# A hybrid decoder layer on one core: first projections by kinds of parts, other buffers for held weights, evictions behind weight splits, and half banks in the last product

## The chip, the cores and the metric

The kernel runs on one core of a Trainium2 chip. The metric is device time in microseconds, the median over several runs. Five engines work side by side, each on its own queue of instructions in program order: TensorE (PE, matmuls and transposes; PEld is its weight load), VectorE (DVE), ScalarE (ACT), GpSimd (POOL) and SyncE (SP, which here only issues DMAs). They wait for each other by semaphores.

## The reference

One layer with a residual stream of 1024 rows of 1024 columns, with 16 learned rows put ahead of it. All is float32.

```python
u = rmsnorm(h, g_pre_mix)
z = u @ w_in                                   # q | k | v | x_rec | y_rec
attn = sliding_window_attention_with_sinks(q, k, v, sinks)      # window 128, 8 heads, 2 kv heads
xr = causal_depthwise_conv(xr, conv_w, conv_b)
hr = rg_lru(xr, w_a, b_a, w_x, b_x, lru_lambda)
rec = gelu(yr) * hr
h = h + rmsnorm(concat([attn, rec]) @ w_out, g_post_mix)
u = rmsnorm(h, g_pre_ffn)
f = square(relu(u @ w_ff1)) @ w_ff2            # 1024 -> 4096 -> 1024
h = h + rmsnorm(f, g_post_ffn)
return h[:, 16:]
```

## The kernel before

**Parts.** Every float32 operand of a matmul is split into a high part (rounded to the matmul's type by ACT, L95 or L116) and a low part (the remainder, by DVE, L98 or L117). A product is three matmuls: high by high (L123), high by low (L124), low by high (L125), all added up in a PSUM bank (`mm3`). The high part of a weight is ready before its low part, since DVE subtracts what ACT wrote.

**Start.** The rows come in four pieces (`ALL`: 272 rows with the 16 learned ones, then three times 256). For each piece `normed` takes the norm (a square with a sum on ACT, L200; two steps on POOL, L158 and the power L164; a multiply on DVE, L202), `transposed` turns it on TensorE into PSUM (L242) and splits it into `u`, and `project` runs the K, V, Q and X columns over it. The results go to sinks: `sink_k` copies K into two arrangements, with casts on ACT (L303) and DVE (L304) and subtractions on DVE (L305). The projections' accumulators take turns on two banks with the tag acc, so a third projection waits until the first one's sink has read its bank. `kl` is zeroed in part by POOL (L298).

**Middle.** Attention, with the other projections placed between its steps (50 to 250 us in the trace), then the recurrence's gates, then the output projection.

**Feed-forward, first product.** Both big products are done by a recursive scheme of seven half-size products in place of eight, with sums and differences of blocks of the weights taken on DVE (`combine`, L789). In `prep_a` piece p loads two blocks of w_ff1, r0 (tag raw) and r1 (tag d, four buffers), takes sums, splits, and writes r1 to DRAM (`s_dram`, by POOL, L834) for a later pass (`fetch_b`). A d buffer is free again only when that write is done. Another operand, t4, is written to DRAM too (L963) and loaded into `ot4` (L1015) for the third pass.

**Feed-forward, second product.** `steps` are 56 pairs (i, q): seven products of eight steps each; a step is 24 matmuls of 512 columns. Step n runs while `prep_2` makes the operands of step n + 1 and `fetch_2` loads w_ff2 for step n + 3 into the tags raw and e (two buffers each). Where the weight is a sum of two blocks, the second one is added either by an accumulating DMA, issued by POOL (L1039), or it is loaded by SP too (L1042) and added by DVE:

```python
if len(wx) == 3 and wx[2] is ADD and raws and (i < 6 or q % 2 == 0):
    nc.gpsimd.dma_start(raws[0], w2v[q, a, b], accum_op=ADD)
    break
```

After each product `evict` adds the four banks to sums in SBUF (L1144, L1147, L1149) in the first four steps of the next product. `finish_early` ends the lower rows (L1094 squares, L1101 scaling, an accumulating DMA from h_dram at L1105). `finish_half` prepares half the columns of the upper rows in the first four steps of the last product. The last three steps (`LAST`) are run row block by row block, and `finish_late` ends each: eviction (L1126), squares on ACT (L1094), L160 and the power L164, a multiply by the gain (L1129), two scalings with the residual (L1131) and two output DMAs (L1134).

**What sets the order.** A scheduler orders each engine's queue by priorities and by its own estimate of the times; `behind(name, ins)` adds an order of one instruction after another on the same engine without a semaphore. `mark` and `urgent` are names for it. Slots (`slot`) with one tag take turns on that tag's buffers, and whoever takes one waits for the last reader or writer of the one before.

Of the kernel before, what the change touches and what calls it, by code (L numbers as in the profile page):

```python
# [37 lines left out]
def hybrid_layer(  # L38
# [76 lines left out]
    def split_scaled(hi, lo, src, scale):  # L115
        nc.scalar.activation(hi, src, AF.Copy, scale=scale)  # L116
        nc.vector.scalar_tensor_tensor(  # L117
            lo, src, scale, f32(hi), op0=ALU.mult, op1=ALU.subtract
        )

    def mm3(dst, lhs, rhs, start, stop):
        (lh, ll), (rh, rl) = lhs, rhs
        nc.tensor.matmul(dst, lh, rh, start=start, stop=False, skip_group_check=True)  # L123
        nc.tensor.matmul(dst, lh, rl, start=False, stop=False, skip_group_check=True)  # L124
        nc.tensor.matmul(dst, ll, rh, start=False, stop=stop, skip_group_check=True)  # L125
# [29 lines left out]
    def rstd_of(ssq_parts, n=P):  # L155
        ms = small.tile([P, 1], F32, name="ms", tag="ms")
        if len(ssq_parts) == 1:
            nc.gpsimd.tensor_scalar(ms[:n], ssq_parts[0], EPS, None, op0=ALU.add)  # L158
        else:
            nc.vector.scalar_tensor_tensor(  # L160
                ms[:n], ssq_parts[0], EPS, ssq_parts[1], op0=ALU.add, op1=ALU.add
            )
        rs = small.tile([P, 1], F32, name="rs", tag="rs")
        nc.gpsimd.tensor_tensor(rs[:n], ms[:n], half_pow[:n], op=ALU.pow)  # L164
        return rs[:n]

# [30 lines left out]
    def norm_rows(src, n):  # L197
        xn = slot("d", [P, D])
        ssq = small.tile([P, 1], F32, name="ssq", tag="ssq")
        nc.scalar.activation(xn[:n], src, AF.Square, scale=RMS_SC, accum_out=ssq[:n])  # L200
        rs = rstd_of([ssq[:n]], n)
        nc.vector.tensor_scalar(xn[:n], src, rs, None, op0=ALU.mult)  # L202
        return xn
# [13 lines left out]

    ALL = [(0, 272), (272, 256), (528, 256), (784, 256)]
    REAL2 = [(16, 512), (528, 512)]

# [14 lines left out]
    def transposed(b, xn):  # L235
        t0, n = ALL[b]
        for kc in range(KC):
            flip[0] += 1
            pt = bank(("pt", "o", "s")[flip[0] % 3])
            o = 0  # L240
            for s, m in xn:
                nc.tensor.transpose(  # L242
                    pt[:, o : o + m], s[:m, kc * P : (kc + 1) * P], ident[:m, :m]
                )
                o += m
            uh, ul = u[kc]
            split_scaled(
                uh[:, t0 : t0 + n], ul[:, t0 : t0 + n], pt[:, :n],
                g_mix_col[:, kc : kc + 1],
            )  # L250

# [25 lines left out]
    wk = split_w(rk, "b")  # L277
    wv = split_w(rv, "b")
    transposed(0, xn)
    wq = split_w(rq)  # L280
    wx = split_w(rx)
# [8 lines left out]

    khh = [slot("b", [P, T], F32R) for _ in range(2)]
    kl = [slot("b", [P, T], F32R) for _ in range(2)]

    vk = [slot("b", [P, 8, P], F32R) for _ in range(2)]
    HALF = (slice(0, HD), slice(HD, P))
    vt = slot("c", [P, TT])
    for h in range(2):
        nc.gpsimd.memset(f32(kl[h][HALF[1 - h]]), 0.0)  # L298
# [43 lines left out]

    q0, sink_q0 = new_q()
    xr0, sink_x0 = new_x("c")
    for b in range(4):
        if b:
            transposed(b, normed(b))
        piece = [ALL[b]]
        project(wk, piece, sink_k)
        project(wv, piece, sink_v)  # L350
        project(wq, piece if b else [(16, 256)], sink_q0)
        project(wx, piece, sink_x0)
# [251 lines left out]
    nc.gpsimd.memset(graw, 0.0)  # L604
# [207 lines left out]
    def prep_a(p, late=None):  # L812
        r0 = slot("raw", [P, 4, 256])
        w1_load(r0, 0, p, 0, 2)
        r1 = slot("d", [P, 4, 256])
        w1_load(r1, 1, p, 0, 2)
        a11, a21, a12, a22 = r0[:, :, LO], r0[:, :, HI], r1[:, :, LO], r1[:, :, HI]
        sums = [
            combine(a22, a21, a22, ALU.add), combine(a21, a11, a21, ALU.subtract)
        ]  # L820
        if late:
            behind(late, *sums)
        hi, lo = pair("ws", [P, 4, 256])
        if p in a11_early:
            split(hi[:, :, HI], lo[:, :, HI], a21)
            first = a11_early[p]
        else:
            split(hi, lo, r0)
            first = hi[:, :, LO], lo[:, :, LO]
        combine(a11, a22, a11, ALU.subtract)  # L830
        hl = slot("e", [P, 2, 4, P], F32R)
        split(hl[:, 0], hl[:, 1], a11)
        combine(a12, a12, a11, ALU.subtract)
        nc.gpsimd.dma_start(s_dram[p], r1)  # L834
        return first, (hl[:, 0], hl[:, 1]), (hi[:, :, HI], lo[:, :, HI])
# [177 lines left out]
    for i in range(2):  # L1013
        for n in range(2):
            nc.sync.dma_start(f32(ot4[i][n]), t4_dram[:, n, 2 * i : 2 * i + 2, :])  # L1015

# [15 lines left out]
    def fetch_2(n):  # L1032
# [4 lines left out]
        for (a, b), tag in zip(wx[:2], tags):  # L1037
            if len(wx) == 3 and wx[2] is ADD and raws and (i < 6 or q % 2 == 0):
                nc.gpsimd.dma_start(raws[0], w2v[q, a, b], accum_op=ADD)  # L1039
                break  # L1040
# [5 lines left out]
    def prep_2(n, tag="ws"):  # L1046
# [3 lines left out]
        if len(raws) == 2:  # L1050
            combine(raws[0], raws[0], raws[1], wx[2])
        wh, wl = pair(tag, [P, 2, 512])
        split(wh, wl, raws[0])
# [11 lines left out]
    ready, raw_2 = {}, {}  # L1065


    done = set()
    for n, p in enumerate(third):
# [13 lines left out]
        product(y4, wc[p][1], ot4, True)  # L1083
# [24 lines left out]
    late = {}  # L1108

    def finish_half(j):  # L1110
# [9 lines left out]
        nc.vector.tensor_tensor(o[:, c], acc[:, c], gffn_b[:, c], op=ALU.mult)  # L1120
        late[j] = h, o, ssq

    def finish_late(j, y):
        h, o, ssq1 = late[j]
        acc, c = facc["0", j], COLS[0]
        nc.vector.tensor_tensor(acc[:, c], y, acc[:, c], op=ALU.add)  # L1126
        ssq0 = squares(o[:, c], acc[:, c], 0)
        rs = rstd_of([ssq0, ssq1])
        nc.vector.tensor_tensor(o[:, c], acc[:, c], gffn_b[:, c], op=ALU.mult)  # L1129
        for c in COLS[::-1]:  # L1130
            nc.vector.scalar_tensor_tensor(  # L1131
                o[:, c], o[:, c], rs, h[:, c], op0=ALU.mult, op1=ALU.add
            )
            nc.sync.dma_start(out[j * P : (j + 1) * P, c], o[:, c])  # L1134
# [3 lines left out]
    def evict(i, j, y):  # L1138
        for half, b, sign in PLAN[i][2]:
# [6 lines left out]
            elif sign > 0:  # L1146
                nc.vector.tensor_tensor(dst, y, dst, op=ALU.add)  # L1147
            else:
                nc.vector.tensor_tensor(dst, dst, y, op=ALU.subtract)  # L1149

    def step_mm(accs, j, q, ops):
        fh, fl, wh, wl = ops
        c = slice(j * P, (j + 1) * P)
        for s_ in range(2):
            mm3(
                accs[j], (fh[:, s_, c], fl[:, s_, c]), (wh[:, s_, :], wl[:, s_, :]),
                q == 0 and s_ == 0, q == 7 and s_ == 1,
            )

# [5 lines left out]
    for n, (i, q) in enumerate(steps):  # L1165
        if n + 3 < len(steps):
            raw_2[n + 3] = fetch_2(n + 3)
        if n + 1 < len(steps):
            ready[n + 1] = prep_2(n + 1, "a" if n + 1 >= len(steps) - LAST else "ws")
        if q == 0:  # L1170
            old = None if i == 0 else accs
            accs = [bank(("acc", "s", "pt", "o")[j]) for j in range(4)]
        if n < len(steps) - LAST:
            for j in range(4):
                step_mm(accs, j, q, ready[n])
            del ready[n]
        if old and q < 4:
            evict(i - 1, q, old[q])
# [5 lines left out]
        if i == 6 and q < 4:  # L1184
            finish_half(q)
    for j in range(4):
        for n in sorted(ready):
            step_mm(accs, j, steps[n][1], ready[n])
        finish_late(j, accs[j])
# [31 lines left out]
```

## Time and profile before

| | us |
|---|---|
| median of 3 runs | 995.67 (993.17 to 998.14) |
| profiled execution | 997.85 |
| its span, first to last instruction | 995.9 |
| TensorE busy | 962.2 |
| VectorE busy | 673.5 |
| ScalarE busy | 502.9 |
| GpSimd busy | 76.5 |

The profiled execution is one run; its own time is its span and some 2 us around it. The busy share of TensorE is high everywhere but at a few places, and these are best found by windows of equal length: the same number of matmuls of one size fits into each, so missing ones show lost time. The column PEclk is the clock that TensorE was granted, as a share of full speed.

### The profile page before, as it was taken

Reading aid. Unit: us, or ns where it says so; the run is one execution under the profiler, and the core shown is the slowest. Engines: PE = TensorE matmul, PEld = TensorE weight load, DVE = VectorE, ACT = ScalarE, POOL = GpSimd, SP = SyncE. Lnnn points to the kernel's source line nnn. Section 1 sums busy time; section 2 is a strip of 40 time slices with the busy share of each in tenths; the row PEclk is TensorE's granted clock in tenths of the full one; section 3 lists DMA queues with packets and bytes.
Section 4 is the critical chain, followed back from the end, with each engine's and each line's share of the span. In section 5 each row is a group of like instructions: output and inputs, shape, how many; then the busy total and the mean of one; then the engine's idle time right before and its main releaser. Section 6 shows DMA issues by size and latency. Waiting matters only on the chain.

```text
span 995.9 us, 12412 instructions
## 1 busy us (share of the span) xinstructions
PE 962.2 (97%) x4734; PEld 804.0 (81%) x4734; DVE 673.5 (68%) x995; ACT 502.9 (50%) x813; POOL 76.5 (8%) x108
## 2 busy tenths in 40 slices
PE   6999999999999999989999999999999899999986
PEld 6999999888788877868888878888888688888764
DVE  6679996756966786655654455476566577688955
ACT  7657573658735554333555555654533344344421
POOL 4000000000021100000000000000111100012121
PEclk9999999999999999989999999999999999999998
DMA  8101001112236455666533354324877866647672
GB/s 281 31 13 53 23 22 43 43 43 64 66 146 191 146 159 180 224 204 205 169 103 104 111 168 127 106 87 125 178 165 177 193 209 195 184 147 223 169 190 85
DMA packets 89371, 133.28 MB, mean 134 GB/s; under 512 B 13752, under 2 KB 52680, under 8 KB 89312
## 3 DMA queue, kind: packets, MB, share of 16 engines
q1 hardware_dynamic: 80704, 110.47, 35.0%
q0 software_dynamic: 8320, 20.97, 10.5%
q10 hardware_dynamic: 288, 1.05, 0.3%
q8 instruction: 37, 0.61, 0.2%
q14 instruction: 22, 0.18, 0.1%
HBM read 113.60 MB, written 18.87 MB: 133 GB/s over the span
## 4 chain that ended last, share of the span: by engine, by line
PE 72%; issue 9%; DVE 7%; DMA 7%; POOL 2%; ACT 2%; SPq 0%; POOLq 0%; DVEq 0%; ACTq 0%
PE ps_acc L124 9%; PE ps_acc L125 9%; PE ps_acc L123 9%; PE ps_pt L124 5%; PE ps_pt L123 5%; PE ps_pt L125 5%; PE ps_s L124 4%; PE ps_s L125 4%; PE ps_s L123 4%; PE ps_o L124 4%; PE ps_o L123 4%; PE ps_o L125 4%; DMA raw<-in_w_ff_dram 2%; DMA d<-in_w_ff_dram 2%; PE ps_o L506 2%
## 5 line engine op out<-in xcount | busy, mean ns | idle before, releaser
L95 ACT CAST ws<-raw 128x1024 fp32r<-128x1024 f32 (+1 forms) x70 | 71.7, 1024 | 124.1 <-PE ps_o L124 43.4
L98 DVE TENSOR_TENSOR ws<-raw,ws 128x1024 fp32r<-128x1024 f32 (+1 forms) x71 | 84.7, 1193 | 45.5 <-ACT ws L95 45.3
L123 PE MATMUL ps_acc<-a,ws 128*128 128x256 f32 (+2 forms) x272 | 90.5, 333 | 0.6 <-DVE b L305 0.6
L124 PE MATMUL ps_acc<-a,ws 128*128 128x256 f32 (+2 forms) x272 | 89.8, 330 | 0.0
L125 PE MATMUL ps_acc<-a,ws 128*128 128x256 f32 (+2 forms) x272 | 89.4, 329 | 0.0
L95 ACT CAST ws<-e 128x1024 fp32r<-128x1024 f32 x44 | 46.1, 1047 | 73.0 <-PE ps_o L124 25.0
L98 DVE TENSOR_TENSOR b<-b,b 128x1024 fp32r<-128x1024 f32 (+2 forms) x48 | 57.5, 1199 | 23.3 <-PE ps_o L124 15.7
L98 DVE TENSOR_TENSOR ws<-e,ws 128x1024 fp32r<-128x1024 f32 x44 | 53.8, 1223 | 25.1 <-ACT ws L95 25.0
L95 ACT CAST b<-b 128x1024 fp32r<-128x1024 f32 (+2 forms) x48 | 49.4, 1028 | 36.6 <-DVE b L789 34.5
L164 POOL TENSOR_TENSOR rs<-ms,half_pow 128x1 f32<-128x1 f32 (+1 forms) x33 | 28.3, 861 | 386.6 <-DVE ms L160 385.2
L123 PEld LDWEIGHTS ps_acc<-a,ws 128*128 128x128 f32 x272 | 51.2, 188 | 4.9 <-DVE b L305 0.8
L125 PEld LDWEIGHTS ps_acc<-a,ws 128*128 128x128 f32 x272 | 51.2, 188 | 4.6
L124 PEld LDWEIGHTS ps_acc<-a,ws 128*128 128x128 f32 x272 | 51.2, 188 | 3.9
L124 PE MATMUL ps_acc<-ws,b 128*128 128x512 f32 x110 | 43.6, 397 | 4.4 <-DVE ws L98 4.3
L124 PE MATMUL ps_pt<-ws,b 128*128 128x512 f32 x112 | 44.5, 398 | 0.0
L125 PE MATMUL ps_pt<-ws,b 128*128 128x512 f32 x112 | 44.5, 397 | 0.0
L123 PE MATMUL ps_pt<-ws,b 128*128 128x512 f32 x112 | 44.4, 396 | 0.0
L125 PE MATMUL ps_s<-ws,b 128*128 128x512 f32 x110 | 44.2, 402 | 0.0
L124 PE MATMUL ps_s<-ws,b 128*128 128x512 f32 x110 | 44.2, 402 | 0.0
L123 PE MATMUL ps_s<-ws,b 128*128 128x512 f32 x110 | 43.9, 399 | 0.0
L123 PE MATMUL ps_acc<-ws,b 128*128 128x512 f32 x110 | 43.6, 396 | 0.0
L125 PE MATMUL ps_acc<-ws,b 128*128 128x512 f32 x110 | 43.5, 396 | 0.0
(368 smaller groups left out, 2671.1 us busy)
## 6 DMA issues: line engine op xcount, KB each, us to landing
raw<-in_w_ff_dram SPq DMA_DIRECT2D x64, 512.0 KB, 4.3
e<-in_w_ff_dram SPq DMA_DIRECT2D x44, 512.0 KB, 3.7
d<-in_w_ff_dram SPq DMA_DIRECT2D x16, 512.0 KB, 4.8
s_dram<-d POOLq DMA_DIRECT2D x16, 512.0 KB, 4.2
raw<-in_w_ff_dram POOLq DMA_DIRECT2D x12, 512.0 KB, 5.8
raw<-in_w_in_dram SPq DMA_DIRECT2D x9, 512.0 KB, 3.8
c<-in_x_dram SPq DMA_DIRECT2D x8, 512.0 KB, 8.8
d<-in_x_dram SPq DMA_DIRECT2D x8, 512.0 KB, 5.1
```

What stands on the lines that cost most here:

```text
L95: nc.scalar.copy(hi, src)
L98: low = nc.vector.tensor_tensor(lo, src, f32(hi), op=ALU.subtract).ins
L123: nc.tensor.matmul(dst, lh, rh, start=start, stop=False, skip_group_check=True)
L124: nc.tensor.matmul(dst, lh, rl, start=False, stop=False, skip_group_check=True)
L125: nc.tensor.matmul(dst, ll, rh, start=False, stop=stop, skip_group_check=True)
L164: nc.gpsimd.tensor_tensor(rs[:n], ms[:n], half_pow[:n], op=ALU.pow)
L506: nc.tensor.matmul(po[:, oc : oc + n], v, p_[:, pc : pc + n], start=first and k == 0, stop=last and k == 1, skip_group_check=True,)
```

## The change

- First projections: the memsets of `kl` come first on POOL. For the first piece, `part` runs the products by kind (all high by high, then high by low, then low by high) with K and V on the two banks together; casts of the weights, high and low evictions and two later norms are chained on ACT and DVE in a written order (`chained`); transposes of later pieces are held behind the X projection of the piece before (`done`). The memset of `graw` is held behind the last power.
- `prep_a` puts r1 into tag a instead of d for pieces 2 to 5.
- `ot4` loads both high halves first, and the first product with it runs by parts.
- `fetch_2` uses the accumulating DMA for q % 3 < 2 (i < 6) and for q = 0, 2, 4 (i = 6).
- Evictions are held behind the weight's low split of the step before (`late`); the first one of product 5 stands ahead of the last product's matmuls; `finish_half` runs one step later, its multiply behind the low split; sums of two blocks in the last product too.
- The fourth row block of the last product gets two accumulators of 256 columns, one in a bank of its own; `finish_late` takes it in two halves. For the last two row blocks the squares of the last columns run on DVE (`tensor_tensor_reduce`) with the other half's sum as a start; the multiply by the gain moves to POOL for the first three; the last output DMA goes by ACT's queue.

```diff
+    def part(acc, w, piece, k, last=2):
+        t0, n = piece
+        for kc in range(KC):
+            last_mm[0] = nc.tensor.matmul(
+                acc[:, :n], w[k // 2][:, kc, :], u[kc][k % 2][:, t0 : t0 + n],
+                start=k == 0 and kc == 0, stop=k == last and kc == KC - 1,
...
+    def chained(e, ins):
+        if last[e] is not None:
+            behind(last[e], ins)
+        last[e] = ins.name
...
-    wk = split_w(rk, "b")
-    wv = split_w(rv, "b")
+    wk = high_w(rk, "b")
     transposed(0, xn)
-    wq = split_w(rq)
-    wx = split_w(rx)
+    low_w(wk, rk)
+    wv = high_w(rv, "b")
+    low_w(wv, rv)
+    xn = [(norm_rows(xt[i], P, True), P) for i in (2, 3)]
+    wq = high_w(rq)
+    low_w(wq, rq)
+    wx = high_w(rx)
+    low_w(wx, rx)
...
-            transposed(b, normed(b))
-        piece = [ALL[b]]
...
+            transposed(b, xn if b == 1 else normed(b), done[b])
+        piece = ALL[b]
+        if b == 0:
+            acc = [bank("acc"), bank("acc")]
+            for a, w in zip(acc, (wk, wv)):
+                part(a, w, piece, 0)
+                part(a, w, piece, 1)
+            for a, w, sink in zip(acc, (wk, wv), (sink_k, sink_v)):
+                part(a, w, piece, 2)
+                sink(a[:, : piece[1]], *piece)
+            for w, (t0, n), sink in ((wq, (16, 256), sink_q0), (wx, piece, sink_x0)):
+                acc = bank("acc")
+                for k in range(3):
+                    part(acc, w, (t0, n), k)
+                sink(acc[:, :n], t0, n)
...
-    nc.gpsimd.memset(graw, 0.0)
+    behind(last_pow[0], nc.gpsimd.memset(graw, 0.0).ins)
...
-        r1 = slot("d", [P, 4, 256])
+        r1 = slot("a" if 2 <= p < 6 else "d", [P, 4, 256])
...
-    for i in range(2):
-        for n in range(2):
+    for n in range(2):
+        for i in range(2):
             nc.sync.dma_start(f32(ot4[i][n]), t4_dram[:, n, 2 * i : 2 * i + 2, :])
...
-            if len(wx) == 3 and wx[2] is ADD and raws and (i < 6 or q % 2 == 0):
+            if len(wx) == 3 and wx[2] is ADD and raws and (
+                q % 3 < 2 if i < 6 else q in (0, 2, 4)
+            ):
...
-            combine(raws[0], raws[0], raws[1], wx[2])
+            ins = combine(raws[0], raws[0], raws[1], wx[2])
+            if i == 6:
+                behind(w_low[0], ins)
...
+        if n == 0:
+            product_by_parts(y4, wc[p][1], ot4)
+        else:
+            product(y4, wc[p][1], ot4, True)
...
+        if j > 1:
+            nc.gpsimd.tensor_scalar(ssq, ssq, EPS, None, op0=ALU.add)
+        behind(w_low[0], combine(o[:, c], acc[:, c], gffn_b[:, c], ALU.mult))
...
+        for k, c in enumerate(parts):
+            yield k
+            ins = combine(acc[:, c], y[k], acc[:, c], ALU.add)
+            if k == 1:
+                behind(w_low[0], ins)
+            if j < 2:
+                rs = rstd_of([squares(o[:, c], acc[:, c], 0), ssq])
+                continue
+            part = small.tile([P, 1], F32, name=f"part{k}", tag=f"part{k}")
+            nc.vector.tensor_tensor_reduce(
+                out=o[:, c], in0=acc[:, c], in1=acc[:, c], scale=RMS_SC * RMS_SC,
+                scalar=ssq, op0=ALU.mult, op1=ALU.add, accum_out=part,
+            )
+            ssq = part
+        if j > 1:
+            rs = small.tile([P, 1], F32, name="rs", tag="rs")
+            nc.gpsimd.tensor_tensor(rs, ssq, half_pow, op=ALU.pow)
+        c = COLS[0]
+        if j < 3:
+            nc.gpsimd.tensor_tensor(o[:, c], acc[:, c], gffn_b[:, c], op=ALU.mult)
+        else:
+            combine(o[:, c], acc[:, c], gffn_b[:, c], ALU.mult)
+        for c, eng in zip(COLS[::-1], (nc.sync, nc.scalar)):
...
-                nc.vector.tensor_tensor(dst, y, dst, op=ALU.add)
+                behind(late, combine(dst, y, dst, ALU.add))
...
+            if i == 6:
+                evict(5, 0, old[0][0], late)
+                accs[3] = [accs[3][0][:, :256], bank("acc")[:, :256]]
...
-        if i == 6 and q < 4:
-            finish_half(q)
+        if i == 6 and 1 <= q < 5:
+            finish_half(q - 1)
```

## The prediction

> **What bounds the kernel now.** I read the page first, then busy time by window, then what TensorE waits for, then the engines' timelines around each wait.
>
> ```profile
> PE 962.2 (97%) x4734; PEld 804.0 (81%) x4734; DVE 673.5 (68%) x995; ACT 502.9 (50%) x813; POOL 76.5 (8%) x108
> ```
>
> TensorE is busy 97% of the span, so only its interruptions can be won. The windows size them; columns are PE, PEld, DVE, ACT and POOL busy time with instruction counts, granted clock, DMA share, GB/s.
>
> ```profile
> 600.00:775.00 175.00, 175.00 (x760) 142.34 (x759) 107.70 (x104) 82.97 (x86) 16.97 (x14) 1.00 0.56 139
> 425.00:450.00 25.00, 20.87 (x80) 16.11 (x79) 15.27 (x19) 10.06 (x15) 1.06 (x2) 0.86 0.63 207
> 575.00:600.00 25.00, 22.86 (x97) 17.67 (x96) 14.85 (x17) 15.64 (x17) 0.00 (x0) 1.00 0.58 173
> 775.00:800.00 25.00, 22.47 (x88) 17.10 (x87) 13.23 (x12) 9.78 (x11) 2.40 (x2) 0.93 0.80 203
> 925.00:950.00 25.00, 23.15 (x95) 18.48 (x94) 23.91 (x28) 11.68 (x20) 7.87 (x3) 0.93 0.60 163
> 950.00:975.00 25.00, 22.14 (x88) 17.32 (x87) 11.11 (x10) 5.14 (x5) 2.13 (x2) 0.93 0.71 169
> ```
>
> The first row is undisturbed: 175/760 = 0.230 us for a 512-column matmul, so 108.6 fit into 25 us. The missing ones, times 0.230, are the loss: 6.6 us at 425, 2.7 at 575, 4.7 at 775, 3.1 at 925, 4.7 at 950; together 21.8. The waits behind them:
>
> ```profile
> PE ps_acc L124 <- DVE ws L98: 4.3, 2, 2.5
> PE ps_acc L123 <- ACT ws L95: 3.9, 1, 3.9
> PE ps_acc L123 <- ACT a L95: 2.8, 1, 2.8
> PE ps_pt L124 <- DMA b<-t_dram: 1.8, 2, 1.1
> PE ps_acc L123 <- DVE b L305: 0.6, 1, 0.6
> ```
>
> They account for about 13 us (the first row is two places). The rest is clock:
>
> ```profile
> 427.80:434.60 6.80, 5.07 (x11) 3.58 (x12) 6.04 (x8) 2.15 (x3) 0.53 (x1) 0.50 0.17 47
> 789.60:793.00 3.40, 3.40 (x10) 2.62 (x9) 1.23 (x1) 1.99 (x2) 0.00 (x0) 0.50 0.73 243
> ```
>
> After a wait the granted clock is 0.50 for 3.4 or 6.8 us; 10 matmuls instead of 15 pass in 3.4 us, 1.1 us lost. The Trainium skill (TensorE: Matmul & The Clock Gate, "Part 1: The HAM clock gate") ties the half clock to at least one idle window of about 3.4 us; by that the longest wait at 775–800, 2.5 us, would not have brought it, and the trace, with 0.50 there, disagrees.
>
> **First projections (startup): a gain, and a larger loss.** The memsets of kl move to the front of POOL:
>
> ```profile
> 7.34 0.76 DVE L202 TENSOR_SCALAR d<-c,rs 128x1024 f32<-128x1024 f32 x1 [0.28 <-POOL rs L164]
> 8.87 1.52 DVE L202 TENSOR_SCALAR d<-c,rs 128x1024 f32<-128x1024 f32 x1 [0.77 <-POOL rs L164]
> 8.89 2.38 POOL L298 MEMSET b<- 64x1024 f32 x2
> ```
>
> The second norm multiply took twice the first beside the memset. It gets back 0.76 us; with projections by kinds of parts (high parts first, so that low parts aren't waited for) I take 1.1 earlier at about 21 us.
>
> The loss: the X projection of the first piece takes the K projection's bank, free when sink_k's last subtraction (L305) is done.
>
> ```profile
> 27.15 1.05 ACT L200 ACTIVATE d<-c 128x1024 f32<-128x1024 f32 x1
> 27.34 0.43 DVE L305 TENSOR_TENSOR b<-ps_acc,b 64x256 fp32r<-64x256 f32 x1
> 27.82 0.40 PE L123 MATMUL ps_acc<-a,ws 128*128 128x272 f32 x1 [0.57 <-DVE b L305]
> ```
>
> Before, that subtraction ended at 27.77 and TensorE lost 0.6. In the built changed kernel, ACT has two squares of later norms (1.05 each) and the last two high evictions ahead of sink_k's wide casts; DVE has the two norm multiplies (0.76 each, as at 7.34) ahead of the last cast and subtraction. Counting from TensorE's last transpose before that matmul, at about 25.0 (27.0 less the 1.1 and four transposes, 0.4, now later; the rest is rounding): high eviction 0.4, square 1.2 with its readout, eviction 0.4, square 1.2, cast 0.4; then DVE 0.9, norm 0.76, cast and subtraction 0.9. That is 6.1 to 31.1, less some overlap: a wait of 5.7, where 0.6 was. Then a half-clock window, 1.1 to 2.2. Net: 5.1 + 1.1 - 1.1 and a few tenths of window, **+4.5**. Ends: -1 if the casts are not held, +7.
>
> Further on, graw's memset is held behind the last rs of the fourth piece on POOL; its four loads follow on SP, and ACT's cast of it has evictions behind it. TensorE has projections ahead there: 0, at worst +2.
>
> **r1 of pieces 2 to 5 in "a" instead of "d" (the 425 stall).**
>
> ```profile
> 414.69 5.42 DMA s_dram<-d
> 420.12 6.50 DMA d<-in_w_ff_dram
> 429.48 1.23 DVE ws L98
> ```
>
> The chain: a d buffer must be written to s_dram (5.42) before piece p+2 may load into it (6.50), then the sums. A piece costs TensorE 36 x 0.230 = 8.3. Now four pieces skip the d cycle, and the d loads for pieces 6 and 7 wait only for writes of pieces 0 and 1, long past. Piece 9's chain starts some 8 us earlier, twice the 3.9 us wait. SP stays in order: the d loads stand behind raw loads that wait for low splits. I take **-6.0** of the 6.6 (ends 0 and -6.6). The cycle returns from piece 8 on; at 450–490 it ran without a wait.
>
> **ot4 by parts.** The loads' landing (min, median, max) and the wait row above:
>
> ```profile
> DMA to landing us min/median/max: 2.6/7.0/9.7
> ```
>
> All four are issued together and share bandwidth; TensorE waited for each low half and once for a high one (1.8 + 0.3). Now the low halves are needed eight matmuls (1.8) in, but the second high half two matmuls (0.5) in, where some 1.2 between landings is usual: most of the wait moves there. **-0.6** (0 to -2.7).
>
> **Fewer accumulating DMAs.**
>
> ```profile
> 765.70 1.20 POOL L1039 DMA_DIRECT2D raw<-in_w_ff_dram  x1 [4.91 <-issue]
> ...
> 777.75 1.20 POOL L1039 DMA_DIRECT2D raw<-in_w_ff_dram  x1 [4.75 <-issue]
> 786.01 1.23 DVE L789 TENSOR_TENSOR raw<-raw,e 128x1024 f32<-128x1024 f32 x1 [5.06 <-DMA e<-in_w_ff_dram]
> ```
>
> Three accumulations span 12.05, one every 6.0 us; a step costs TensorE 24 x 0.230 = 5.5: half a microsecond of lead lost per step, gone at 785. With six of eight, 12 x 6.0 = 72 against 16 x 5.5 = 88. The four other steps cost DVE 1.23 each, where it is 62% busy (first window row), and a second SP load. **-4.7** (0 to -4.7).
>
> **Last product: evictions behind weights, half banks, halves a step later.**
>
> ```profile
> 932.55 0.68 DVE L1149 TENSOR_TENSOR a<-a,ps_acc 128x512 f32<-128x512 f32 x1
> 940.74 1.22 DVE L98 TENSOR_TENSOR ws<-e,ws 128x1024 fp32r<-128x1024 f32 x1
> 950.74 7.24 DMA raw<-in_w_ff_dram
> 958.66 9.57 DMA raw<-in_w_ff_dram
> ```
>
> Eight evictions (about 0.6 each) and a combine stood ahead of the low split at 940.74; two now do. At 958 a load (7.24) and an accumulation (9.57) in series fed step 6; now two plain loads. By my count from step 48's start, the last three steps' high parts are ready 2 to 3 us before their matmuls. But step 2's accumulation (load 5, accumulate 6 after a buffer freed) leaves ACT and DVE about 0. So **-6.0** of 7.8 (ends 0 and -7.8). The 48 split matmuls: **+0.3**.
>
> **Tail.** The last rows' chain runs from TensorE's end to the output.
>
> ```profile
> 986.12 0.86 POOL L164 TENSOR_TENSOR rs<-ms,half_pow 128x1 f32<-128x1 f32 x1 [3.14 <-DVE ms L160]
> 986.34 0.40 PE L125 MATMUL ps_o<-a,b 128*128 128x512 f32 x1
> 988.35 0.68 DVE L1126 TENSOR_TENSOR a<-ps_o,a 128x512 f32<-128x512 f32 x1
> 991.08 1.41 DVE L1131 SCALAR_TENSOR_TENSOR a<-a,rs,d 128x512 f32<-128x512 f32 x2 [0.44 <-POOL rs L164]
> 15.53 0.96 POOL L604 MEMSET e<- 128x1024 f32 x1 [4.25 <-DVE ws L98]
> 942.78 5.48 POOL L164 TENSOR_TENSOR rs<-ms,half_pow 128x1 f32<-128x1 f32 x1 [10.60 <-DVE ms L160]
> 942.54 1.89 DVE L1120 TENSOR_TENSOR a<-a,a 128x512 f32<-128x512 f32 x3
> ```
>
> TensorE ends at 986.7, DVE at 992.5: 5.8 later. After, DVE's work from the third row block's eviction on sums to 7.6, and POOL has three products of 512 columns as well; a 1024-column memset took 0.96, so 0.6 to 1.5 each. DVE's last eviction stands behind a scaling that waits for POOL's third product. The rs at 942.78 took 5.48 where 0.86 is usual, while DVE ran without a pause: POOL gets its turn when DVE stops. Beside each other, TensorE's end to DVE's is 6.1; taking turns, 9.2. Ends -1 and +4; **+2.0**. The Trainium skill (SBUF — State Buffer, "SBUF: two separate sides") says that a DVE instruction with two SBUF inputs and a GpSimd one that reads SBUF lock each other out for a whole instruction; by that rule the tail is nearer +3.4. It speaks against this part, and the 5.48 agrees.
>
> **Sum**: +4.5 - 6.0 - 0.6 - 4.7 - 6.0 + 0.3 + 2.0 = -10.5. The profiled run took 997.85 (span 995.9), 2.2 above the median 995.67; I forecast the median, **985.2**. A measurement can tell about 0.5%, 5 us.
>
> **Rivals.**
> - Startup is not held up and the tail breaks even: -10.5 - 4.5 - 2.0 = -17, 978.7. For it: ACT and DVE may overlap better than I count. Against: the order is written into the queues. Chance 0.17.
> - The last product gains nothing and POOL takes turns with DVE in the tail: -10.5 + 6.0 + 2.0, 993.2. For: the 5.48 and the 9.57; against: fewer evictions in front. 0.17.
> - The "a" buffers only move the 425 stall, the change not doing what it says there: -10.5 + 6.0, 991.2. For: from piece 8 on the cycle is the old one. 0.11.
> - Slower: uncovered attention. The built order moves projections among the attention steps of 50–250.
>
> ```profile
> L467 DVE CUSTOM_DVE_ANT_0 c<-ps_s,mask,nsink x64: 443/480/484, 53.0 to 194.3; 128x256 f32<-128x256 f32 x64
> L467 DVE DVE_READ_ACCUMULATOR2_ANT negm<- x64: 71/82/85, 53.4 to 194.7; 128x1 f32 x64
> ```
>
>   64 reductions over eight rounds (a head pair and half of the rows each): 8 x 0.56 = 4.5 us of DVE a round; with the exponentials and scalings that follow I put a round's chain at 9, an estimate, twice that. If projections run out early, two uncovered rounds already give -10.5 + 18, 1003.2; it decides from the second round on. Against: in both orders projections reach to the end of attention. 0.09.
> - The forecast: 0.46.
>
> Range 978 to 996: below it lies part of the first rival, above it the last. Faster 0.70 (forecast, first rival, the edge of the middle two), same 0.20, slower 0.10.
>
> **What would show it.** Right: a TensorE wait of 5 to 6 us near 25–31 ended by DVE L357; no matmul missing at 425–450 and 775–800; POOL products between DVE instructions at the end, TensorE's end to the span's end about 11 against 9.2. Wrong: no wait near 30, new waits on ACT or DVE in 50–250, or a stall for e or raw after 940.

## The result and the profile after

The changed kernel took 986.95 us (median of 5 runs, 986.01 to 989.44); the kernel before took 997.98 (5 runs on the same chip, 993.17 to 998.64). The ratio is 0.9905, 95% interval 0.9878 to 0.9932: about 1% less time, and the interval leaves out 1. The forecast was 985.2. The profiled execution has a span of 984.1 against 995.9, 11.8 less.

The page's busy times and the windows of the changed kernel, columns as before:

```profile
PE 955.5 (97%) x4782; PEld 803.2 (82%) x4782; DVE 680.7 (69%) x1002; ACT 502.3 (51%) x809; POOL 71.9 (7%) x108
```

```profile
25.00:50.00 25.00, 19.44 (x142) 19.38 (x142) 11.63 (x32) 9.15 (x25) 1.88 (x4) 0.80 0.07 21
425.00:450.00 25.00, 25.00 (x109) 20.27 (x109) 17.25 (x22) 10.63 (x16) 2.13 (x4) 1.00 0.79 256
575.00:600.00 25.00, 25.00 (x109) 20.06 (x108) 15.67 (x17) 15.06 (x16) 0.00 (x0) 1.00 0.66 208
775.00:800.00 25.00, 25.00 (x109) 20.30 (x109) 17.49 (x16) 12.28 (x14) 1.21 (x1) 1.00 0.79 228
925.00:950.00 25.00, 23.37 (x122) 19.54 (x121) 20.09 (x23) 9.14 (x13) 3.53 (x3) 1.00 0.68 168
950.00:975.00 25.00, 23.15 (x126) 19.68 (x124) 18.43 (x21) 6.33 (x11) 6.78 (x7) 1.00 0.32 105
```

Three holes are closed: 109 matmuls at 425, 575 and 775, where 80, 97 and 88 stood. A new one is open at 25–50: 142 matmuls, at a clock of 0.80 (before, the same window had x207 at 1.00). In the last two rows the counts include 256-column matmuls and can't be set beside the old ones; what TensorE waits for there says more. The changed kernel's waits, the first row from 20 to 45 us, the others from 925 to 975:

```profile
PE ps_acc L237 <- DVE b L357: 5.6, 1, 5.6
...
PE ps_acc L124 <- ACT ws L95: 0.9, 1, 0.9
PE ps_acc L125 <- DVE ws L98: 0.8, 1, 0.8
```

The first is the wait for the K projection's bank; the others are what is left in the last product. To put all stretches on one scale I priced every matmul and transpose started up to a point at the undisturbed interval of its form (0.230 us for 512 columns) and subtracted that from the time at that point. It is the time that TensorE has lost by then, in us (the levels hang on the price of each form, the differences between the kernels much less):

| by | before | after | difference in the stretch | forecast for it |
|---|---|---|---|---|
| 50 | 17.1 | 22.6 | +5.5 (startup) | +4.5 |
| 300 | 28.8 | 35.4 | +1.0 (attention) | 0 |
| 500 | 41.5 | 40.3 | -7.7 (r1 in "a") | -6.0 |
| 700 | 45.0 | 41.4 | -2.5 (ot4) | -0.6 |
| 900 | 51.4 | 43.6 | -4.1 (accumulating DMAs) | -4.7 |
| TensorE's last end | 986.73 | 973.15 | -5.8 (last product, split matmuls included) | -5.7 |
| TensorE's end to the span's end | 9.2 | 10.95 | +1.8 (tail) | +2.0 |

These add up to -11.8.

### The profile page after: what moved, and what is told of

Its sections match the earlier page's. It is cut to its first block, busy times and chain, and to the rows that moved or that the text cites. A ratio compares the mean times of both kernels' runs of the same rounds, so it can differ in the third digit from the quotient of the medians.

```text
span 984.1 us, 12519 instructions
## 1 busy us (share of the span) xinstructions
PE 955.5 (97%) x4782; PEld 803.2 (82%) x4782; DVE 680.7 (69%) x1002; ACT 502.3 (51%) x809; POOL 71.9 (7%) x108
## 4 chain that ended last, share of the span: by engine, by line
PE 87%; DVE 5%; DMA 4%; ACT 2%; issue 1%; POOL 1%; POOLq 0%; SPq 0%; DVEq 0%; ACTq 0%
PE ps_acc L125 10%; PE ps_acc L124 10%; PE ps_acc L126 10%; PE ps_s L126 6%; PE ps_s L124 6%; PE ps_s L125 6%; PE ps_pt L124 6%; PE ps_pt L126 6%; PE ps_pt L125 6%; PE ps_o L125 5%; PE ps_o L124 5%; PE ps_o L126 5%; DMA raw<-in_w_ff_dram 2%; PE ps_o L577 2%; PE ps_pt L566 1%
## 5 line engine op out<-in xcount | busy, mean ns | idle before, releaser
L98 DVE TENSOR_TENSOR ws<-raw,ws 128x1024 fp32r<-128x1024 f32 (+1 forms) x71 | 84.7, 1194 | 54.7 <-ACT ws L95 54.5
L124 PE MATMUL ps_acc<-a,ws 128*128 128x256 f32 (+2 forms) x256 | 85.8, 335 | 0.1
L125 PE MATMUL ps_acc<-a,ws 128*128 128x256 f32 (+2 forms) x256 | 85.3, 333 | 0.0
L126 PE MATMUL ps_acc<-a,ws 128*128 128x256 f32 (+2 forms) x256 | 84.9, 332 | 0.0
L98 DVE TENSOR_TENSOR b<-b,b 128x1024 fp32r<-128x1024 f32 (+2 forms) x48 | 57.6, 1201 | 26.1 <-PE ps_o L125 18.6
L95 ACT CAST ws<-e 128x1024 fp32r<-128x1024 f32 x42 | 43.8, 1043 | 57.6 <-PE ps_o L125 27.6
L95 ACT CAST b<-b 128x1024 fp32r<-128x1024 f32 (+2 forms) x48 | 49.4, 1030 | 43.5 <-DVE b L860 41.5
L98 DVE TENSOR_TENSOR ws<-e,ws 128x1024 fp32r<-128x1024 f32 x42 | 51.4, 1223 | 21.4 <-ACT ws L95 21.4
L126 PEld LDWEIGHTS ps_acc<-a,ws 128*128 128x128 f32 x256 | 48.2, 188 | 4.4
L124 PEld LDWEIGHTS ps_acc<-a,ws 128*128 128x128 f32 x256 | 48.3, 189 | 4.2 <-ACT c L391 0.3
L125 PEld LDWEIGHTS ps_acc<-a,ws 128*128 128x128 f32 x256 | 48.2, 188 | 3.7
L125 PE MATMUL ps_acc<-ws,b 128*128 128x512 f32 (+1 forms) x120 | 46.5, 388 | 1.1 <-DVE ws L98 1.1
L124 PE MATMUL ps_acc<-ws,b 128*128 128x512 f32 (+1 forms) x120 | 46.3, 386 | 0.9 <-ACT ws L95 0.9
L169 POOL TENSOR_TENSOR rs<-ms,half_pow 128x1 f32<-128x1 f32 (+1 forms) x31 | 21.7, 704 | 347.3 <-DVE ms L165 345.9
L126 PE MATMUL ps_acc<-ws,b 128*128 128x512 f32 (+1 forms) x120 | 46.2, 385 | 0.0
L124 PE MATMUL ps_s<-ws,b 128*128 128x512 f32 x110 | 43.4, 394 | 0.0
L125 PE MATMUL ps_s<-ws,b 128*128 128x512 f32 x110 | 43.3, 394 | 0.0
L126 PE MATMUL ps_s<-ws,b 128*128 128x512 f32 x110 | 43.2, 393 | 0.0
```

The source lines that it names most:

```text
L95: nc.scalar.copy(hi, src)
L98: low = nc.vector.tensor_tensor(lo, src, f32(hi), op=ALU.subtract).ins
L126: last_mm[0] = nc.tensor.matmul(dst, ll, rh, start=False, stop=stop, skip_group_check=True).ins.name
L169: last_pow[0] = nc.gpsimd.tensor_tensor(rs[:n], ms[:n], half_pow[:n], op=ALU.pow).ins.name
```

## The experiments

Each is an edit of the changed kernel. The medians of different batches belong to different chips, with the kernel before at 997.76, 998.44, 997.46 and 996.53, so ratios are compared.

**The startup undone.** The whole first bullet of the change goes back (chains, `part`, early memsets, held transposes, the graw order).

```diff
-        if b == 0:
-            acc = [bank("acc"), bank("acc")]
...
+        project(wk, [piece], sink_k)
+        project(wv, [piece], sink_v)
+        project(wq, [piece] if b else [(16, 256)], sink_q0)
```

> The changed kernel with the first projections as before (three matmuls by row block, POOL's memsets behind the first norms, no chains, no hold on the transposes, graw's memset free). Theory A, the startup costs more than it gains (by 50 us the changed kernel has lost 5.5 us more than the one before): the wait of 5.7 us at 24.8 goes, the rest stays, the span falls by 5 to 6 us from 984.1 to about 978.5. Theory B, the startup's loss is made up for later, since TensorE has work enough in attention whose partners catch up: the span changes by less than 2 us.

979.21 us, ratio 0.9843 (0.9806 to 0.9879), span 975.4. The windows at 25–50 of this kernel:

```profile
25.00:50.00 25.00, 24.43 (x207) 24.14 (x206) 16.73 (x42) 15.26 (x39) 2.48 (x6) 1.00 0.11 28
```

All 207 are back and the change without its startup part is better: that part costs. Of the 8.7 us of span, some 5 are there by 50 us (17.5 lost against 22.6) and 1.0 more by 300, where a wait of 0.4 us for `DVE c L98` in the attention comes with the new startup. Another 2.3 come in small pieces up to 900, which I haven't located.

**The bank.** The X projection of the first piece goes to bank "s", which is free; nothing else moves.

```diff
             for w, (t0, n), sink in ((wq, (16, 256), sink_q0), (wx, piece, sink_x0)):
-                acc = bank("acc")
+                acc = bank("acc" if w is wq else "s")
```

> The changed kernel, but the first piece's X projection takes a bank of the tag s in place of the two of the tag acc. Theory A, it was the K projection's bank, held by sink_k, that TensorE waited for: the wait of 5.7 us at 24.8 and the half clock after it go, and with the 1.1 us that the order by kinds gains the span falls to 977 to 979. Theory B, it was the amount of work on DVE and ACT (evictions, norms, casts) and any bank would do: a wait of 3 us or more comes back a few matmuls later, and the span falls by less than 3 us.

982.12 us, ratio 0.9852 (0.981 to 0.9894), span 979.3. Its window, and what TensorE still waits for there:

```profile
25.00:50.00 25.00, 23.34 (x194) 22.69 (x194) 16.20 (x40) 14.76 (x36) 3.27 (x7) 1.00 0.10 27
```

```profile
PE ps_acc L124 <- ACT a L116: 1.2, 1, 1.2
```

The 5.6 us wait is gone and the clock is whole. By 50 us 15.9 are lost, 1.2 less than before the change: the new startup (early memsets, projections by kinds of parts and chains; no run takes them apart) does gain, and the shared bank turned the gain into a loss. The span fell by 4.8 rather than 6.7 because the last product lost 2.8 us more in this run (below).

**The casts first.** The evictions of the second piece and the norms of later pieces are held behind K's last cast and subtraction; the bank is shared as in the change.

```diff
+            if b == 1:
+                behind(k_sunk[0], high[0])
+                behind(k_sunk[1], high[1])
...
+        elif hold:
+            behind(k_sunk[0], ins)
```

> The changed kernel, but the second piece's evictions and the later norms are held behind sink_k's last cast on ACT and its last subtraction on DVE. Theory A, the order on the two queues made the wait: X begins at about 26 in place of 30.6, a wait of 1 to 2 us is left, the clock stays whole, and the span falls by 4 to 6 us. Theory B (work, not order): the second piece's K projection waits for its evictions instead, 3 us or more at about 29, and the span falls by less than 3 us.

981.25 us, ratio 0.9853 (0.9813 to 0.9892). Its wait there:

```profile
PE ps_acc L241 <- DVE b L364: 2.2, 1, 2.2
```

5.6 became 2.2, with one window of half clock in place of three, and 17.4 us lost by 50. The span, 981.0, fell by 3.1 where theory A said 4 to 6, and the clock did not stay whole; theory B's wait for the second piece's evictions is not to be seen. So the order of casts and norms on ACT and DVE made the wait long, as the forecast counted; the sharing of the bank makes that a wait remains.

**r1 back in "d".**

```diff
-        r1 = slot("a" if 2 <= p < 6 else "d", [P, 4, 256])
+        r1 = slot("d", [P, 4, 256])
```

> The changed kernel with r1 in the tag d for all pieces. Theory A, the a buffers removed the 425 stall: the wait for ACT and DVE at about 420 comes back with 3.9 us and a half-clock window, and the span rises by 6 to 8 us. Theory B, the stall went since the stage starts at another phase: no wait above 1 us there, the span the same within 2 us.

994.0 us (10 runs), ratio 0.9977 (0.9952 to 1.0002). Its window, wait and clock after the wait:

```profile
425.00:450.00 25.00, 20.98 (x79) 16.14 (x78) 11.45 (x16) 7.47 (x11) 0.57 (x2) 0.86 0.69 226
...
435.50:442.30 6.80, 5.98 (x13) 4.31 (x14) 5.16 (x7) 1.53 (x4) 0.53 (x1) 0.50 0.27 70
```

```profile
PE ps_acc L124 <- ACT ws L95: 3.6, 1, 3.6
```

The stall of 3.6 us and 6.8 us of half clock return, with 79 matmuls, where 80 stood before the change. The buffers alone carry that term, and they don't only move it: 49.1 us are lost by 500 here, 40.3 in the changed kernel. The rival that said so falls.

**Accumulating DMAs as before.**

```diff
-                q % 3 < 2 if i < 6 else q in (0, 2, 4)
+                i < 6 or q % 2 == 0
```

> The changed kernel with the accumulating DMA for every sum of i < 6 and every even q of i = 6, as before. Theory A, accumulations every 6.0 us against 5.5 us of TensorE a step use up the lead: the wait near 775 comes back, 4 to 5 us with its half clock, and in the last product a wait near 955 of up to 3 us. Theory B, the stage begins with more lead in the changed kernel, since TensorE no longer waits at 425 and 584 while the loads go on: no wait above 1 us before 800.

991.27 us, ratio 0.9924 (0.9895 to 0.9953), span 989.9. Two of its windows:

```profile
775.00:800.00 25.00, 23.69 (x103) 18.92 (x102) 15.20 (x15) 12.04 (x14) 1.19 (x1) 1.00 0.78 222
925.00:950.00 25.00, 22.54 (x103) 18.49 (x102) 20.70 (x24) 8.70 (x13) 3.43 (x3) 0.86 0.60 151
```

Six matmuls (1.4 us) are missing at 775 where 21 were missing before the change, and no half clock follows. From 700 to 900 this kernel loses about 1 us more than the changed one, where the kernel before loses 4.1 more. The rest of its longer span is lost in the last product (about 6, against 2.5) and in the tail (12.8, against 10.95). So a stall returns at the place predicted, but far below theory A's 4 to 5 us: fewer accumulations alone don't account for what the stretch gained, and which other edit gave the rest no run shows. There is no stall for step 6 of the last product, although its accumulating DMA is back.

**ot4: the order of loads and the order of parts**, one undone each time.

```diff
# parts undone, loads as changed
-        if n == 0:
-            product_by_parts(y4, wc[p][1], ot4)
-        else:
-            product(y4, wc[p][1], ot4, True)
+        product(y4, wc[p][1], ot4, True)
# loads undone, parts as changed
-    for n in range(2):
-        for i in range(2):
+    for i in range(2):
+        for n in range(2):
```

> The changed kernel with its order of the four ot4 loads (both high halves first), but with the first product by row block (high, low, low for each). Theory A, the order by parts is what hides the low halves: TensorE waits about 2 us or more in all at 583, as the second matmul needs a low half that is loaded third. Theory B, the order of the loads lands them sooner (last one 7.5 us after its issue, before 9.7): waits below 1.5 us in all.

> The changed kernel with the first product by parts, but with the four ot4 loads in the order of before (high and low of the first pair, then of the second). Theory A, by parts hides the low halves, but the second high half lands third: a wait of 1 to 2 us. Theory B, the loads' order sets how fast they land: the last lands 9 to 10 us after its issue and the waits are 2 us or more. If neither waits, the order by parts alone was enough.

983.32 us (ratio 0.9844, 0.9816 to 0.9873) and 989.37 (0.9905, 0.9876 to 0.9934). From issue to landing of the four loads (min, median, max): before, changed, parts undone, loads undone:

```profile
DMA to landing us min/median/max: 8.6/8.8/9.7
```

```profile
DMA to landing us min/median/max: 6.0/6.2/7.5
```

```profile
DMA to landing us min/median/max: 6.7/7.0/7.9
```

```profile
DMA to landing us min/median/max: 8.0/8.2/9.1
```

TensorE's waits with parts undone, and with loads undone:

```profile
PE ps_pt L125 <- DMA b<-t_dram: 1.1, 1, 1.1
```

```profile
PE ps_pt L1091 <- DMA b<-t_dram: 2.0, 1, 2.0
```

In both, theory B came nearer: 1.1 us of wait with the loads as changed, 2.0 with the old order of loads. With the halves of one kind loaded together all four land 1.2 to 2 us sooner, and by parts the low ones aren't needed until later; the wait goes only with both. All twelve kernels with the new order of loads had the last one after 7.0 to 7.9 us, the two with the old order after 9.1 and 9.7. Both kernels' times differ from the changed one's mostly by what the last product lost in that run (0.1 and 4.8).

**The orders in the last product undone.** Evictions, sums and halves aren't held behind low splits, and `finish_half` starts at step 0.

```diff
-                behind(late, combine(dst, y, dst, ALU.add))
+                combine(dst, y, dst, ALU.add)
...
-        if i == 6 and 1 <= q < 5:
-            finish_half(q - 1)
+        if i == 6 and q < 4:
+            finish_half(q)
```

> The changed kernel without the orders of the evictions, of the last product's sums and of finish_half's multiply behind the weight's low splits, and with finish_half from step 0 on; loads, half banks and the eviction that stands first stay. Theory A, the low split behind eight evictions made the wait at 940: it comes back with 2 us or more and half a clock window, and the last steps' loads, whose buffers come free later, wait again near 960 for up to 3 us. Theory B, the accumulating DMA alone made it: as in the changed kernel, 2.1 us in all.

983.73 us, ratio 0.9848 (0.982 to 0.9877). Its wait and window there:

```profile
PE ps_acc L125 <- DVE ws L98: 2.0, 1, 2.0
```

```profile
925.00:950.00 25.00, 23.03 (x125) 19.56 (x124) 23.36 (x27) 11.78 (x21) 9.41 (x5) 1.00 0.66 161
```

2.2 us are lost in the last product, much as with the orders (2.5), but not by the same wait. The changed kernel waits for step 2, whose weights an accumulating DMA brings late. Here that DMA is issued at 922.22, 8 us before step 1 begins, and TensorE waits within step 1 for the low split of its weights, which stands behind eight evictions. VectorE of the changed kernel, then VectorE and POOL of this one:

```profile
928.77 1.22 DVE L98 TENSOR_TENSOR ws<-e,ws 128x1024 fp32r<-128x1024 f32 x1
```

```profile
923.80 0.68 DVE L860 TENSOR_TENSOR a<-a,ps_acc 128x512 f32<-128x512 f32 x1
...
927.99 0.68 DVE L860 TENSOR_TENSOR a<-ps_o,a 128x512 f32<-128x512 f32 x1
...
931.99 1.21 DVE L98 TENSOR_TENSOR ws<-e,ws 128x1024 fp32r<-128x1024 f32 x1
...
922.22 1.21 POOL L1121 DMA_DIRECT2D raw<-in_w_ff_dram  x1 [11.53 <-ACT b L95]
```

With the orders the split begins 1.5 us after ACT begins the high part (927.25), without them 7.1 us after (924.92). So the wait of theory A is back with 2.0 us, though without its half clock and without a wait near 960: the orders do what they were made for. Their gain doesn't show in the total, since the changed kernel pays about as much for its late DMA; why that DMA is early here the traces don't tell.

**Output writes behind the loads.** In the changed kernel the chain that ends in the waits near 937 runs through an output write on SP that waits for its own accumulating DMA, with weight loads queued behind it. Here it is issued behind the next step's loads.

```diff
-        nc.sync.dma_start(out[t * P : (t + 1) * P, :], o)
+        return lambda: behind(
+            w2_load[0], nc.sync.dma_start(out[t * P : (t + 1) * P, :], o).ins
+        )
```

> The output write of each finished row block in the second half of the feed-forward is issued behind the next step's weight loads on SyncE's queue, not ahead of them; everything else is the changed kernel. Theory A (that write, which waits for its own accumulating DMA and holds the loads behind it, is what is late in the last product): the chain that ends in the wait near 937 starts up to 6 us earlier, the idle time of 2.1 us there goes to under 0.5, the time to about 985 us. Theory B (the loads wait for their buffers and for each other, not for the write): a wait of 2 to 5 us stays in 925 to 975 us and the time is 986 to 988 us.

989.2 us, ratio 0.9918 (0.9891 to 0.9945). The accumulating DMA of step 2 on POOL, changed kernel and this one, and this one's wait:

```profile
929.71 1.18 POOL L1121 DMA_DIRECT2D raw<-in_w_ff_dram  x1 [13.06 <-DMA raw<-in_w_ff_dram]
```

```profile
928.66 1.19 POOL L1123 DMA_DIRECT2D raw<-in_w_ff_dram  x1 [20.17 <-DVE ws L98]
```

```profile
PE ps_acc L124 <- ACT ws L95: 2.2, 1, 2.2
```

The accumulation is only 1.05 us earlier, and so is the last product itself (its first matmul at 924.7, against 925.9); the wait stays, as the load ahead of it needs a buffer that the low split frees. Theory A falls. The kernel is slower than the changed one in the last product (5.3 lost, against 2.5) and in the tail, 12.6 us here; the next experiment bears on the tail.

**The tail**, in two steps: GpSimd's three products back on VectorE; then the whole end as before the change.

```diff
-        if j < 3:
-            nc.gpsimd.tensor_tensor(o[:, c], acc[:, c], gffn_b[:, c], op=ALU.mult)
-        else:
-            combine(o[:, c], acc[:, c], gffn_b[:, c], ALU.mult)
+        combine(o[:, c], acc[:, c], gffn_b[:, c], ALU.mult)
# second kernel, besides
-        return HALVES if i == 6 and j == 3 else COLS[:1]
+        return COLS[:1]
...
-            nc.vector.tensor_tensor_reduce(
...
+            rs = rstd_of([squares(o[:, c], acc[:, c], 0), ssq])
```

> The three products with the output norm's weight that the change put on GpSimd at the end are made by VectorE, all else as changed. Theory A (VectorE and GpSimd reading SBUF at once cost each other time at the end): the 512-column reduce that took 1.77 us beside a GpSimd product falls to about 1.2, the products cost VectorE about 0.6 us each, and the stretch from TensorE's last end to the span's end goes from 10.95 to about 10 us, the time to about 986 us. Theory B (the products were really taken off VectorE's chain): the stretch grows by up to 1.9 us to 11 to 13 us and the time is 987 to 989 us.

> The end of the last product as before the change: squares on ScalarE, whole 512-column banks for the fourth row block, products on VectorE, both output writes from SyncE; all else as changed. Theory A (the change's new end is 1.8 us longer because it was rebuilt, as the two traces say): the stretch from TensorE's last end to the span's end falls from 10.95 to about 9.2 us and the time to about 985.2 us. Theory B (the longer end comes from where the last stretch stands against the DMA queues, or the old end only hides its cost inside TensorE's time): the stretch may fall, but the time stays at 986 to 988 us or rises.

987.58 us (ratio 0.9901, 0.9874 to 0.9928) and 983.23 (0.9868, 0.9838 to 0.9899). From TensorE's end to the span's end 10.0 and 9.5 us, against 10.95, near theory A's 10 and 9.2. The same reduce beside GpSimd's product (changed kernel, DVE and POOL) and without it (products on VectorE):

```profile
970.34 1.77 DVE L1227 CUSTOM_DVE_ANT_0 a<-a,late 128x512 f32<-128x512 f32 x1
...
970.28 1.28 POOL L1237 TENSOR_TENSOR a<-a,a 128x512 f32<-128x512 f32 x1
```

```profile
975.13 0.75 DVE L1227 CUSTOM_DVE_ANT_0 a<-a,late 128x512 f32<-128x512 f32 x1
```

The reduce loses 1.02 of GpSimd's 1.28 us. VectorE makes a product in 0.69, so moving one to GpSimd saves 0.69 and costs up to 1.0 where the two meet. In the kernel with the late writes a 256-column reduce was caught too:

```profile
976.57 1.48 DVE L1231 CUSTOM_DVE_ANT_0 a<-a,late 128x256 f32<-128x256 f32 x1
...
976.37 1.41 POOL L1241 TENSOR_TENSOR a<-a,a 128x512 f32<-128x512 f32 x1
```

It took 0.48 where POOL was quiet. The Trainium skill (SBUF — State Buffer, "SBUF: two separate sides") has a VectorE instruction with two SBUF inputs and a GpSimd one that reads SBUF lock each other out for a whole instruction. These lengths agree to some 0.2 us: a reduce of 0.75 that waits for the product's end would show as 1.97, one of 0.48 as 1.69. How much the products cost depends on what they meet: the new end takes 10.9 us in seven kernels, 12.6 and 12.8 in the two where a 256-column reduce was caught (late writes, and accumulating DMAs as before), and 10.0 with the orders undone, where GpSimd still makes them but no reduce was held up (0.74 and 0.48). That is no longer than with all of them on VectorE. The time of the first of the two kernels is no better than the changed one's because its last product lost 6.2 us.

**Three edits together.** The bank "s", the old end, and no accumulating DMA for step 2 of the last product.

```diff
-                acc = bank("acc")
+                acc = bank("acc" if w is wq else "s")
...
-                q % 3 < 2 if i < 6 else q in (0, 2, 4)
+                q % 3 < 2 if i < 6 else q in (0, 4)
...
+        return COLS[:1]
...
+            rs = rstd_of([squares(o[:, c], acc[:, c], 0), ssq])
```

> Three edits of the changed kernel together: the X projection of the first piece goes to bank s, so that TensorE does not wait for bank acc near 25 us; the end of the last product is the one from before the change; and the weights of the last product's step q = 2 come by two loads and a sum on VectorE instead of an accumulating DMA. Theory A (the accumulating load of step 2 is the late link of the last product, and the three costs add): no wait of over 1 us in 925 to 975 us, so 2.2 to 3.7 us less there, 6.7 us less from the startup (15.9 instead of 22.6 us lost by 50 us) and 1.4 us less from the end, together 10 to 12 us under the changed kernel's span of 984.1 us: a span of 972 to 974 us and a time of 974 to 977 us. Theory B (buffers and DMA bandwidth set the last product's pace, and an accumulating DMA is only where the wait shows): a wait of 2 to 5 us stays in 925 to 975 us at another step, the span is 976 to 979 us and the time 978 to 982 us.

975.19 us (5 runs, 974.4 to 976.01), ratio 0.9783 (0.9758 to 0.9808), span 973.4: faster than both kernels. Its windows:

```profile
25.00:50.00 25.00, 23.29 (x194) 22.64 (x193) 16.19 (x41) 14.70 (x36) 3.27 (x7) 1.00 0.09 23
...
900.00:925.00 25.00, 25.00 (x109) 20.30 (x109) 20.09 (x20) 9.79 (x12) 1.83 (x2) 1.00 0.73 212
925.00:950.00 25.00, 25.00 (x109) 20.27 (x109) 23.23 (x25) 10.35 (x14) 1.20 (x1) 1.00 0.73 209
```

No matmul is missing in the last product, and 0.1 us is lost from 925 on. Step 2's weights now need two loads side by side and a sum of 1.22 us on VectorE, which is busy 23.23 of 25: little more can be put there. Theory A held. The bank and the old end were run alone too, step 2's edit wasn't, so its share is read from the windows and not from a ratio. One trace wouldn't show it, since two kernels that keep the accumulation also lost only 0.1 in the last product. But the five runs of this kernel lie within 1.6 us of span (972.6 to 974.2), where the four with the bank alone spread over 7.0 and the four with the old end alone over 5.1: the swing is gone as well.

## Why the prediction was right, and where its steps were not

The forecast of -10.5 stood against -11.8 in the profiled spans and -11.0 in the medians.

- **Startup, +4.5; measured +5.5.** The wait was forecast at 5.7 and is 5.6, and its cause is the one counted. The sum was a slip: its terms, 5.1 + 1.1 - 1.1 and a few tenths, come to 5.1 or more and not to 4.5. ACT and DVE of the changed kernel just ahead of it:

```profile
25.07 1.05 ACT L209 ACTIVATE d<-c 128x1024 f32<-128x1024 f32 x1
...
26.47 1.05 ACT L209 ACTIVATE d<-c 128x1024 f32<-128x1024 f32 x1
...
29.06 0.37 ACT L355 CAST b<-ps_acc 64x256 fp32r<-64x256 f32 x1 [1.19 <-DVE b L357]
```

```profile
27.40 0.75 DVE L215 TENSOR_SCALAR d<-c,rs 128x1024 f32<-128x1024 f32 x1
...
28.95 0.73 DVE L215 TENSOR_SCALAR d<-c,rs 128x1024 f32<-128x1024 f32 x1
...
30.14 0.43 DVE L357 TENSOR_TENSOR b<-ps_acc,b 64x256 fp32r<-64x256 f32 x1
```

  Two squares stand ahead of K's wide casts and two norm multiplies ahead of its wide casts and subtractions, and the last subtraction ends where TensorE starts again, at 30.6. What was mis-sized is the clock: one window, 1.1 to 2.2 us, was allowed, and there were three.

```profile
26.40:29.80 3.40, 0.00 (x0) 0.00 (x0) 3.31 (x8) 2.18 (x6) 1.78 (x4) 0.50 0.10 30
29.80:33.20 3.40, 2.58 (x11) 2.58 (x12) 1.98 (x8) 0.41 (x2) 0.00 (x0) 0.50 0.00 0
33.20:36.60 3.40, 3.40 (x17) 3.40 (x16) 0.00 (x0) 0.14 (x1) 0.00 (x0) 0.50 0.00 0
```

  Between 31 and 37 us the loss grew from 19.2 to 21.8, 2.6 us, where before it grew by 0.3. That is one execution: in eight other kernels with this startup the same wait of 5.6 us brought two windows (seven kernels) or one (one kernel), and the loss by 50 us was 0.2 to 1.2 us smaller. The gain of the earlier part was some 1.7 and not 1.1.
- **Attention, 0; measured +1.0.** It comes with the new startup, as undoing that showed. The rival of uncovered rounds (+18) is not to be seen.
- **r1 in "a", -6.0; measured -7.7** by 500, of which 1.3 lie before 400, where small waits went as well. The mechanism is shown by its undoing.
- **ot4, -0.6; measured -2.5.** The step that failed: I kept the spacing of the landings of before. The order of the loads itself brought the last landing from 9.7 to 7.5 us, so that the second high half wasn't late.
- **Accumulating DMAs, -4.7; measured -4.1.** The size is right, the reason (lead lost at half a microsecond a step) is shown in part only: with the accumulations back, about 1 us of the 4.1 came back, and without half clock. That the other 3 belong to this term is not shown; to that extent its agreement is luck.
- **Last product, -6.0 and +0.3; measured -5.8.** Right in size. Its first reason is shown by the undoing: without the orders a wait of 2.0 us for a low split behind eight evictions is back. Its second, the accumulation that fed step 6, isn't: that DMA came back with the old accumulations and brought no stall. The caveat holds: step 2's accumulation, which leaves about nothing to spare, is what the changed kernel still loses, and without it the wait is gone.
- **Tail, +2.0; measured +1.8.** VectorE ended 7.8 us after TensorE, between the 6.1 and 9.2 counted, since it and GpSimd took turns in part. How often they meet differs between kernels with the same end (10.0 to 12.8 us), so the closeness of this number is partly luck.

Not settled: what the last product loses swings between 0.1 and 6.2 us over kernels whose code there is the same, or nearly so (0.1 with r1 in "d", 5.3 with the bank "s"). How late the accumulation for step 2 is goes with it. Counted from the first matmul of the last product, POOL issues it 0.8 us after in the two kernels that lost 0.1 (r1 in "d", ot4 with the parts undone) and 3.0 to 6.0 us after in the nine that lost some 2 to 6; only with the orders undone is it earlier, and there the loss has the other cause. The last kernel has no such DMA. Why it is later in one run than in another the traces don't tell. For the same reason the ratios of the experiments on other parts differ by up to 0.6% that isn't theirs, and their verdicts are read at their own place in the trace.

## What to carry to other kernels

When an accumulator's bank is reused, count all that stands on the evicting engines ahead of the last read: the gain of a better order on TensorE turned into a loss through two squares and two norm multiplies, and a free bank gave it back. A DMA that accumulates onto a load is two transfers in series (for step 2 of the changed kernel 4.7 and then 7.2 us); use it where there is lead and load both blocks side by side where there is none. Moving a small product to GpSimd beside VectorE work with SBUF inputs can cost VectorE more than it saves.

## What the runs showed of the hardware

- Half clock came in lengths of 3.4, 6.8 and 10.2 us, and no length of the wait decides it: waits of 2.0 us passed at 1.00 in two places (ot4 with the loads undone, the last product with the orders undone), while one of 1.8 us at 940 before the change was followed by half clock from 943.2 to 946.6, and the same wait of 5.6 us in the startup brought 10.2, 6.8 or 3.4 us of it in nine kernels. The Trainium skill (TensorE: Matmul & The Clock Gate, "Part 1: The HAM clock gate") calls the window free-running, about 3.4 us long, and ties the half clock to at least one that is idle. The lengths and the role of chance fit that; that a whole idle window is needed doesn't fit the 1.8 us.
- Four loads issued together landed up to 2 us sooner (the last after 9.1 and 9.7 us in two kernels, after 7.0 to 7.9 in twelve) when halves with the same place in the second index of the source were asked for one after the other.
